# Two projection DMAs in place of four, and five stores in place of three, in a FiLM layer kernel

## Chip, cores and metric

One core of a Trainium2 chip. The metric is the device time of one execution in microseconds (us). All runs quoted are of the fast state, with a granted clock of 1.00. The same kernel differs by up to 0.4% between jobs on different chips (84.04 to 84.38 us for the kernel before), so each experiment is compared with runs of the kernel before from its own job.

## The reference

```python
# x 32 x 512 x 256, conditioning 32 x 64, gamma_proj and beta_proj 64 x 256, all float32
gamma = conditioning @ gamma_proj
beta = conditioning @ beta_proj
return (x * (1 + gamma[:, None, :]) + beta[:, None, :]).astype(np.float32)
```

It reads 16.78 MB of x and writes 16.78 MB; everything else is small.

## The kernel before

Each of the 128 partitions holds 128 rows of x (a quarter of one batch item, 128 KB). SyncE issues the loads, ScalarE issues everything else that is a DMA. VectorE takes 11 of every 16 rows, GpSimd the other 5.

```python
LOADS = {0: [8, 8, 8, 8, 32, 32, 26, 6]}
STORES = {0: (64, 96, 128)}
GROUP = 16
ON_DVE = 11
# ... (pools cut)
nc.scalar.dma_start(out=cond_s, in_=conditioning)
gbproj = consts.tile([2 * cond_dim, dim], f32)      # rows alternate: gamma, beta, gamma, ...
half = cond_dim // 2
for h, proj in enumerate((gamma_proj, beta_proj)):
    for c0 in (0, half):
        nc.scalar.dma_start(out=gbproj[2 * c0 + h : 2 * (c0 + half) : 2, :],
                            in_=proj[c0 : c0 + half, :])
# ... (the loads of x, one per entry of LOADS, on nc.sync)
# ... (conditioning transposed and repeated on PE; gb_p = gamma | beta for each partition in PSUM;
#      ScalarE copies 1 + gamma and beta to gb_s in SBUF for GpSimd)
held = consts.tile([P, 1], f32)
# ...
for r0 in range(0, ROWS, GROUP):
    # ... (v: 11 rows for VectorE, w: 5 rows for GpSimd; g_p, b_p, g_s, b_s repeated over rows)
    nc.vector.scalar_tensor_tensor(out=v, in0=rows(g_p, nv), scalar=1.0, in1=v, op0=ALU.add, op1=ALU.mult)
    nc.gpsimd.tensor_tensor(out=w, in0=w, in1=rows(g_s, nw), op=ALU.mult)
    nc.vector.tensor_add(out=v, in0=v, in1=rows(b_p, nv))
    nc.gpsimd.tensor_tensor(out=w, in0=w, in1=rows(b_s, nw), op=ALU.add)
    if s == 0 and r0 + GROUP == STORES[0][0]:
        nc.scalar.copy(out=held, in_=slabs[-1][:, ROWS - LOADS[SLABS - 1][-1] - 1, 0:1])   # the gate
    for e0, e1 in zip((0,) + STORES[s], STORES[s]):
        if r0 < e1 <= r0 + GROUP:
            nc.scalar.dma_start(out=o_v[s, :, e0:e1, :], in_=xs[:, e0:e1, :])
```

The copy to `held` reads row 121, which the load before the last one brings. It keeps ScalarE from issuing any store until then.

## Time and profile before

| what | value |
|---|---|
| time, median of 3 runs | 84.04 us (84.01 to 84.16) |
| span of the profiled run | 82.3 us |
| VectorE, GpSimd busy | 61%, 56% |
| both DMA queues together, share of 16 engines | 96.5% |
| last load packet ends, first store packet starts (trace) | 42.4 us, 42.1 us |
| last store packet ends (trace) | 81.1 us |

The prediction below shows the lines that carry this. Three lines that it uses but does not show are from the timeline (start, length, engine, line, operation, and the idle time before it with what ended it):

```profile
3.12 6.79 DMA gbproj<-in_beta_proj_dram
```

```profile
10.04 2.04 PE L94 MATMUL gb_p<-gbproj,cond_T 128*128 128x256 f32 x4 [4.37 <-DMA gbproj<-in_beta_proj_dram]
...
58.78 3.09 DVE L121 TENSOR_TENSOR xs<-xs,gb_p 128x2816 f32<-128x2816 f32 x1
```

The first is from the chain that ended last: the last projection DMA takes 6.79 us for 32 KB, since it shares the engines with loads. The second and third frame the computing: it cannot begin before gb_p, and VectorE is done at 58.78 + 3.09 = 61.87 us, 20 us before the end.

### The profile page before, as it was taken

The numbers are of one execution on the slowest core, as the hardware profiler recorded it, in microseconds if no ns is written. First come the engines' busy times: TensorE is split into PE (matmuls) and PEld (weight loads), VectorE is DVE, ScalarE is ACT, GpSimd is POOL, SyncE is SP. The second block draws the span as 40 slices with busy tenths as digits, with TensorE's granted clock in tenths as the row PEclk, the third lists the DMA queues.
The fourth block names the chain that finished last, engine by engine and source line by source line (L and its number), as shares of the span: only waits on it lengthen the run. The fifth ranks groups of instructions, "written<-read, shape, count | busy, mean of one in ns | idle before, by whom it ended". The sixth has DMA issues, their size and how long they took to land.

```text
span 82.3 us, 140 instructions
## 1 busy us (share of the span) xinstructions
PE 3.3 (4%) x8; PEld 2.1 (3%) x8; DVE 50.1 (61%) x23; ACT 2.1 (3%) x4; POOL 46.4 (56%) x22
## 2 busy tenths in 40 slices
PE   0050180000000000000000000000000000000000
PEld 0040140000000000000000000000000000000000
DVE  1040007999999999999999999999990000000000
ACT  0140012000000000000000000000000000000000
POOL 2000008999999999999999999999700000000000
DMA  2999999799889989999999928999955995998890
GB/s 48 331 426 396 401 418 597 303 462 510 382 382 510 430 350 446 414 427 414 397 689 510 510 127 382 510 510 510 510 255 255 510 510 255 510 510 382 382 510 0
DMA packets 1824, 33.69 MB, mean 409 GB/s; under 512 B 288, under 2 KB 416, under 8 KB 544
## 3 DMA queue, kind: packets, MB, share of 16 engines
q1 hardware_dynamic: 1152, 16.78, 48.7%
q10 hardware_dynamic: 672, 16.92, 47.8%
HBM read 16.92 MB, written 16.78 MB: 409 GB/s over the span
## 4 chain that ended last, share of the span: by engine, by line
DVE 52%; DMA 8%; issue 8%; ACTq 3%; PE 2%; ACT 1%
DVE xs L118 30%; DVE xs L121 23%; DMA gbproj<-in_beta_proj_dram 8%; PE gb_p L94 2%; ACTq L55 2%; ACTq L49 0%; ACT gb_s L98 0%; ACT gb_s L101 0%
## 5 line engine op out<-in xcount | busy, mean ns | idle before, releaser
L120 POOL TENSOR_TENSOR xs<-xs,gb_s 128x1280 f32<-128x1280 f32 x8 | 23.1, 2887 | 11.5 <-ACT gb_s L98 11.5
L118 DVE SCALAR_TENSOR_TENSOR xs<-gb_p,xs 128x2816 f32<-128x2816 f32 x8 | 24.7, 3084 | 6.8 <-ACT gb_s L101 6.8
L121 DVE TENSOR_TENSOR xs<-xs,gb_p 128x2816 f32<-128x2816 f32 x8 | 24.7, 3088 | 0.3
L122 POOL TENSOR_TENSOR xs<-xs,gb_s 128x1280 f32<-128x1280 f32 x8 | 23.1, 2885 | 0.6
L94 PE MATMUL gb_p<-gbproj,cond_T 128*128 128x256 f32 x4 | 2.0, 666 | 4.4 <-DMA gbproj<-in_beta_proj_dram 4.4
L82 DVE COPY wide<-cond_s 32x64 f32<-32x64 f32 x2 | 0.3, 182 | 2.8 <-DMA cond_s<-in_conditioning_dram 2.8
L84 PE MATMUL cond_T_p<-rident,wide 32*128 32x128 f32 x4 | 1.2, 456 | 4.5 <-DVE rident L72 4.5
L98 ACT ACT_TABLE_LOAD x1 | 1.3, 1283 | 3.8 <-issue 3.8
L94 PEld LDWEIGHTS gb_p<-gbproj,cond_T 128*128 128x128 f32 x4 | 1.2, 323 | 4.8 <-issue 4.6
L87 DVE COPY cond_T<-cond_T_p 128x128 f32<-128x128 f32 x2 | 0.6, 292 | 1.0 <-PE cond_T_p L84 0.9
L84 PEld LDWEIGHTS cond_T_p<-rident,wide 32*128 32x128 f32 x4 | 0.9, 319 | 4.4 <-DVE rident L72 4.4
L125 ACT COPY held<-xs 128x1 f32<-128x1 f32 x1 | 0.2, 191 | 28.2 <-DMA xs<-in_x_dram 28.2
L81 DVE MEMSET wide<- 32x128 f32 x2 | 0.3, 165 | 0.8 <-PEq L145 0.8
L98 ACT ACTIVATE gb_s<-gb_p 128x256 f32<-128x256 f32 x1 | 0.4, 383 | 7.1 <-PE gb_p L94 7.1
L101 ACT COPY gb_s<-gb_p 128x256 f32<-128x256 f32 x1 | 0.4, 367 | 0.0
masks.py:197 POOL MEMSET ident<- 32x32 f32 x1 | 0.1, 114 | 0.3 <-POOLq L145 0.3
masks.py:199 POOL TENSOR_SCALAR_AFFINE_SELECT ident<-ident 32x32 f32<-32x32 f32 x1 | 0.2, 202 | 0.1
L145 POOL MEMSET const-float32-0.0<- 128x1 f32 x1 | 0.1, 104 | 0.2 <-issue 0.2
L72 DVE COPY rident<-ident 32x128 f32<-32x128 f32 x1 | 0.2, 208 | 0.0
L145 POOL MEMSET const-bfloat16-1.0<- 128x1 bf16 x1 | 0.1, 107 | 0.0
L145 POOL MEMSET const-uint8-127<- 128x1 uint8 x1 | 0.1, 107 | 0.0
L145 POOL MEMSET const-float32-1.0<- 128x1 f32 x1 | 0.1, 104 | 0.0
## 6 DMA issues: line engine op xcount, KB each, us to landing
xs<-in_x_dram SPq DMA_DIRECT2D x2, 4096.0 KB, 22.0
out_dram<-xs ACTq DMA_DIRECT2D x2, 4096.0 KB, 20.8
xs<-in_x_dram SPq DMA_DIRECT2D x4, 1024.0 KB, 8.4
xs<-in_x_dram SPq DMA_DIRECT2D x1, 3328.0 KB, 32.9
xs<-in_x_dram SPq DMA_DIRECT2D x1, 768.0 KB, 33.9
gbproj<-in_gamma_proj_dram ACTq DMA_DIRECT2D x2, 32.0 KB, 6.0
gbproj<-in_beta_proj_dram ACTq DMA_DIRECT2D x2, 32.0 KB, 6.6
cond_s<-in_conditioning_dram ACTq DMA_DIRECT2D x1, 8.0 KB, 3.1
```

The source lines that it names most:

```text
L55: nc.scalar.dma_start(out=gbproj[2 * c0 + h : 2 * (c0 + half) : 2, :], in_=proj[c0 : c0 + half, :])
L81: nc.vector.memset(wide, 0.0)
L84: nc.tensor.matmul(t_p, lhsT=wide.rearrange("b k h -> b (k h)"), rhs=rident, start=True, stop=True)
L87: nc.vector.tensor_copy(out=t_s, in_=t_p)
L94: nc.tensor.matmul(p_t[:, h * dim : (h + 1) * dim], lhsT=cond_T[h][:, s * P : (s + 1) * P], rhs=gbproj, start=True, stop=True)
L98: nc.scalar.activation(out=s_t[:, :dim], in_=p_t[:, :dim], func=mybir.ActivationFunctionType.Identity, bias=1.0, scale=1.0)
L101: nc.scalar.copy(out=s_t[:, dim:], in_=p_t[:, dim:])
L118: nc.vector.scalar_tensor_tensor(out=v, in0=rows(g_p, nv), scalar=1.0, in1=v, op0=ALU.add, op1=ALU.mult)
L120: nc.gpsimd.tensor_tensor(out=w, in0=w, in1=rows(g_s, nw), op=ALU.mult)
L121: nc.vector.tensor_add(out=v, in0=v, in1=rows(b_p, nv))
L122: nc.gpsimd.tensor_tensor(out=w, in0=w, in1=rows(b_s, nw), op=ALU.add)
L145: nc = _bacc.Bacc("TRN2", target_bir_lowering=False, num_devices=1)
```

## The change

The intent: fewer DMAs ahead of the computing, each over all partitions, and stores in smaller pieces, so that the first can go early and the last is short.

```diff
-    STORES = {0: (64, 96, 128)}
+    STORES = {0: (32, 64, 96, 112, 128)}
...
-    half = cond_dim // 2
-    for h, proj in enumerate((gamma_proj, beta_proj)):
-        for c0 in (0, half):
-            nc.scalar.dma_start(out=gbproj[2 * c0 + h : 2 * (c0 + half) : 2, :],
-                                in_=proj[c0 : c0 + half, :])
+    nc.scalar.dma_start(out=gbproj[0::2, :], in_=gamma_proj)
+    nc.scalar.dma_start(out=gbproj[1::2, :], in_=beta_proj)
```

## The prediction

> **What bounds the kernel now.** I read the page first: busy time by engine, the DMA queues, then the chain of work that ended last.
>
> ```profile
> span 82.3 us, 140 instructions
> ...
> PE 3.3 (4%) x8; PEld 2.1 (3%) x8; DVE 50.1 (61%) x23; ACT 2.1 (3%) x4; POOL 46.4 (56%) x22
> ...
> q1 hardware_dynamic: 1152, 16.78, 48.7%
> q10 hardware_dynamic: 672, 16.92, 47.8%
> HBM read 16.92 MB, written 16.78 MB: 409 GB/s over the span
> ...
> DVE 52%; DMA 8%; issue 8%; ACTq 3%; PE 2%; ACT 1%
> ```
>
> No compute engine is full: VectorE 61%, GpSimd 56%. The two DMA queues (q1 carries the loads of x, q10 the stores, the conditioning and the projections) sum to 48.7 + 47.8 = 96.5% of the time of 16 engines. That is 79.4 of 82.3 us; the remaining 2.9 us are the start (the first read begins at about 1.8 us) and the end. The chain names VectorE with 52%, and here it misleads: it runs back from the last instruction that computes (VectorE's, which ends at 58.78 + 3.09 = 61.87 us) and says nothing of the 20 us of transfers after it.
>
> Next I asked the DMA view for stretches in which nearly all packets have one size: 43 to 61 us (the 64-row store, 64 KB a packet), 62 to 81 us (32-row stores, 32 KB), 10 to 12 us (8-row loads, 8 KB).
>
> ```profile
> DMA packets 112, 7.34 MB, mean 408 GB/s; under 512 B 0, under 2 KB 0, under 8 KB 0
> q10 hardware_dynamic: 112, 7.34, 94.2%
> out_dram<-xs ACTq DMA_DIRECT2D x1, 4096.0 KB, 22.1
> ```
>
> ```profile
> DMA packets 267, 7.86 MB, mean 414 GB/s; under 512 B 27, under 2 KB 27, under 8 KB 27
> q10 hardware_dynamic: 267, 7.86, 96.2%
> out_dram<-xs ACTq DMA_DIRECT2D x1, 4096.0 KB, 19.5
> ```
>
> ```profile
> DMA packets 119, 0.84 MB, mean 422 GB/s; under 512 B 16, under 2 KB 16, under 8 KB 16
> q1 hardware_dynamic: 119, 0.84, 101.7%
> ```
>
> Share x 16 engines x length of the stretch / packets is the time of one packet. 64 KB: 0.942 x 16 x 18 / 112 = 2.422 us. 32 KB: 0.962 x 16 x 19 / 240 = 1.218 us (267 packets less 27 tiny ones that report completion). 8 KB: 1.017 x 16 x 2 / 103 = 0.316 us. (A packet counts in the slice where it starts, hence a share above 100%, and the jagged digits of the page's DMA row, which are not pauses.) The last row of the second fence is the final store: 4 MB need 8 x 1.218 = 9.7 us of each engine, but it took 19.5 us from issue to landing. It stood about 10 us in the queue behind the store before it. So the stores were ready before the DMA engines could take them.
>
> Last, the timeline around the turn from loading to storing.
>
> ```profile
> 40.95 0.19 ACT L125 COPY held<-xs 128x1 f32<-128x1 f32 x1 [28.18 <-DMA xs<-in_x_dram]
> 41.19 21.10 ACTq L129 DMA_DIRECT2D out_dram<-xs  x3
> ```
>
> ScalarE, which issues all stores, waits 28.18 us for row 121 of x, which is in the last load but one. The stores start right after, at 41.19 us, though rows 0 to 63 were finished by 37.4 us. The copy to `held` is a gate: no store before nearly all loads are in.
>
> **What the Trainium skill says.** "DMA: Bandwidth & Descriptors", section "Issuing engines are not separate DMA queues": transfers from any issuing engine share the same 16 DMA engines and interleave. The trace agrees: the two queues together make 96.5%, never much over 100%. The same page, "Where 436 GB/s comes from": the ports allow about 435 GB/s. The trace has 32 KB in 1.218 us on each of 16 engines, 430 GB/s; this kernel is at that ceiling while it streams. "Trace Analysis", section "DMA Optimizations": splitting DMAs may let some start sooner, "If DMA engines are generally idle". Here they are not idle, so the page gives the change no gain. "DMA: Bandwidth & Descriptors", section "Rules for kernel authors": 1 MiB or more per DMA over 128 partitions for the most bandwidth. The new stores have 4, 4, 4, 2 and 2 MB, all above that.
>
> **The change part by part.**
>
> *Projections.* Two DMAs of 64 rows in place of four of 32 rows, the same 128 packets of 1 KB, from the same ScalarE queue. Removed: two issues (0.51 to 0.73 us each in the tile view of gbproj, so ScalarE is free about 1.2 us earlier) and two completion packets per engine. Before, the last of the four was issued at 3.1 us and landed at 9.9 us, because each small packet takes turns with an 8 KB load packet of 0.316 us. Per engine there were 4 x (2 data + 1 completion) = 12 turns; now there are 2 x (4 + 1) = 10. Saving about 2 x 0.32 = 0.6 us, so I put the gb_p matmuls at 9.2 to 9.5 us instead of 10.0, and VectorE's end at about 61.2 instead of 61.9 us. The gain to VectorE can be at most about 1.7 us anyway: rows 32 to 63 land at about 23.3 us (issued at 5.5, 17.8 us to landing), and VectorE takes them at 25.05 now. What is it worth at the end? Nothing: the last store has some 10 us of slack already, and the 0.13 MB of projections move either way. Fewer completion packets are worth a few tens of ns.
>
> *Loads.* Untouched in size and order. In the built kernel (the instruction order with its waits) each DMA takes one of eight completion semaphores in turn; two DMAs fewer ahead of the loads means that the fourth and fifth load need not wait for the conditioning and the first load, so SyncE issues them some us earlier. The engines had queued loads at that time (q1 at 93.8% and q10 at 8.4% from 5 to 10 us), so this moves no byte earlier.
>
> *The gate.* It moves in the source to the first store, but is still one copy that waits for row 121, and the instruction order shows it in the same place on ScalarE, ahead of all stores. So the 32-row store, ready at 25 us, still goes at about 41.2 us.
>
> *Stores.* Three become five. Per DMA engine (8 of the 128 partitions): rows 0 to 63 were 8 packets of 64 KB and become 16 of 32 KB: 16 x 1.218 - 8 x 2.422 = +0.11 us. Rows 64 to 95 stay. Rows 96 to 127 were 8 of 32 KB and become 16 of 16 KB. No 16 KB packet is in the trace; from 2.422 and 1.218 the fixed part of a packet is 0.014 us and 32 KB cost 1.204 us, so 16 KB are an estimated 0.616 us (the same line gives 0.315 for 8 KB, measured 0.316). 16 x 0.616 - 8 x 1.218 = +0.11 us. Completion packets: 16 DMAs in all before (1 + 4 + 8 + 3) and 16 after (1 + 2 + 8 + 5), no difference. Two more issues of 0.34 us on ScalarE hide under transfers.
>
> Does the queue ever run dry? With stores from 42.2 us at 9.7 us per 32 rows, it needs rows 64 to 95 by 61.7, rows 96 to 111 by 71.4, rows 112 to 127 by 76 us. VectorE has them by 49.6, 55.7 and 61.9 us. Never.
>
> Sum: 84.04 + 0.22 - up to 0.1 from the start = **84.2 us**.
>
> **The rivals.**
>
> 1. *The tail shrinks.* If the end is VectorE's end plus the last store's time, then a 2 MB store in place of 4 MB saves 5 us (half of 9.7), or 10 us if one halves the 19.5. For it: VectorE's place in the chain, and that the last store is issued when it ends. Against it: those 19.5 us are half queueing. It would make 74 to 79 us.
> 2. *Stores start earlier* and overlap with loads. For it: rows 0 to 31 are done at 25 us. Against: the gate, and DMA engines at 99.3% between 13.7 and 41 us; starting earlier would only push loads back. It would make 84 us, perhaps worse from starved compute.
> 3. *VectorE's earlier start reaches the end*: 83.4 us. Against: the 10 us of slack.
> 4. *Small packets or a queue hiccup cost more* than 12 to 14 ns each, for instance if 16 KB stores ran at 5% less: 0.5 us on 9.7, making 84.7 us. The 8 KB loads on the line of the others speak against.
>
> **Range and chances.** The mechanism leaves only tenths of a us. Runs of before span 84.01 to 84.16. I take 83.9 to 84.6: the low end allows a somewhat cleaner start, the high end rival 4. A move of 2% (1.7 us) either way needs rival 1, or a stall that no view shows: 1% each.
>
> **What would show it.** Right: queue shares still sum to about 96%, with 16 KB packets near 0.616 us and 32 KB ones at 1.218; the `held` copy again near 41 us and the first store straight after; gb_p matmuls 0.5 to 1 us earlier; VectorE's end earlier with the span unchanged; the last store taking well over its own 4.9 us (an estimate, 8 x 0.616) to land, some 20 us. Wrong: a last store that lands about 5 us after its issue (rival 1), store packets among the loads before 40 us (rival 2), stretches of the storing stage with fewer packets in flight, or loads that end later than 42.9 us because the early issue of loads holds up something.

## The result, and the profile after

The changed kernel took 84.05 us (median of 6 runs, 83.93 to 84.16), the kernel before in the same rounds 84.11 us (6 runs, 84.01 to 84.31). The ratio is 0.999, with a 95% interval of 0.9973 to 1.0007: the same. A ratio here is the mean time of one kernel's fast runs over that of the other's of the same rounds, so it is not quite the ratio of the medians.

The page of the changed kernel, with the queue lines that answer to those of before (packets, MB, share of 16 engines' span):

```profile
span 82.3 us, 141 instructions
...
q1 hardware_dynamic: 1152, 16.78, 48.3%
q10 hardware_dynamic: 928, 16.92, 48.2%
```

The sum is 96.5% again, but it is made up differently. The loads' queue fell from 48.7 to 48.3% (0.4% of 82.3 us = 0.33 us), the stores' queue rose from 47.8 to 48.2%, by the same amount. 256 more packets (928 against 672) are 16 more on each DMA engine.

The DMA view of 71 to 81 us, where only the new 16 KB packets run:

```profile
DMA packets 302, 4.19 MB, mean 419 GB/s; under 512 B 46, under 2 KB 46, under 8 KB 46
...
q10 hardware_dynamic: 302, 4.19, 98.7%
```

0.987 x 16 x 10 us / 256 packets = 0.617 us for one of 16 KB, where 0.616 was estimated. The queue is full to the end.

The timeline, with the rows that answer to those shown of before:

```profile
9.10 2.05 PE L91 MATMUL gb_p<-gbproj,cond_T 128*128 128x256 f32 x4 [3.41 <-DMA gbproj<-in_beta_proj_dram]
...
40.70 0.19 ACT L122 COPY held<-xs 128x1 f32<-128x1 f32 x1 [28.87 <-DMA xs<-in_x_dram]
...
57.85 3.09 DVE L118 TENSOR_TENSOR xs<-xs,gb_p 128x2816 f32<-128x2816 f32 x1
```

gb_p comes 0.94 us earlier and VectorE ends 0.93 us earlier, at 60.94 us. The gate opens at 40.70 instead of 40.95 us; the first store follows at 40.92 us. The span does not move. And the last store, issued at 61.0 us (DMA view of 60.5 to 61.5 us; operation, KB, us from issue to landing):

```profile
out_dram<-xs ACTq DMA_DIRECT2D x1, 2048.0 KB, 20.4
```

It has half the bytes of the last store before, and lands no sooner after its issue (19.5 us then): it queues for some 15 us.

The trace's own packet records show where the two terms lie. The last load packet ends at 42.12 us instead of 42.36 us, so loading ends 0.24 us earlier. From the first store packet to the last it is 39.29 instead of 39.01 us, so storing takes 0.28 us longer. The two cancel. These are single traces: in all six with three stores this length is 39.0 to 39.1 us, in the two with five stores and undelayed computing 39.2 and 39.3 us, so the stores' term is about 0.2 us.

Why loading got shorter is in the DMA view of 6 to 9 us, when the projections' 1 KB packets run between the 8 KB packets of the loads. Before, then after:

```profile
DMA packets 294, 1.19 MB, mean 396 GB/s; under 512 B 64, under 2 KB 161, under 8 KB 161
```

```profile
DMA packets 287, 1.28 MB, mean 428 GB/s; under 512 B 48, under 2 KB 142, under 8 KB 142
```

Fewer bytes were moved in these 3 us before. In the packet records 84 of the 8 KB packets took 0.33 to 0.39 us before, between 6.5 and 9.2 us, in place of 0.31 us. After, none in that time is over 0.33 us.

### The profile page after: what moved, and what is told of

It is laid out like the page before. It is cut to its first block, busy times and chain, and to the rows that moved or that the text cites. A ratio compares the mean times of both kernels' runs of the same rounds, so it can differ in the third digit from the quotient of the medians.

```text
span 82.3 us, 141 instructions
## 1 busy us (share of the span) xinstructions
PE 3.3 (4%) x8; PEld 2.1 (3%) x8; DVE 50.1 (61%) x23; ACT 2.1 (3%) x4; POOL 46.4 (56%) x22
## 3 DMA queue, kind: packets, MB, share of 16 engines
q1 hardware_dynamic: 1152, 16.78, 48.3%
q10 hardware_dynamic: 928, 16.92, 48.2%
## 4 chain that ended last, share of the span: by engine, by line
DVE 52%; DMA 9%; issue 8%; PE 3%; ACTq 1%; ACT 1%
DVE xs L115 30%; DVE xs L118 23%; DMA gbproj<-in_beta_proj_dram 9%; PE gb_p L91 3%; ACTq L52 1%; ACTq L49 0%; ACT gb_s L95 0%; ACT gb_s L98 0%
## 5 line engine op out<-in xcount | busy, mean ns | idle before, releaser
L117 POOL TENSOR_TENSOR xs<-xs,gb_s 128x1280 f32<-128x1280 f32 x8 | 23.1, 2888 | 10.5 <-ACT gb_s L95 10.5
```

## The experiments

My theory after the result: the DMA engines are full, so only their work counts. The five stores add 0.2 to 0.3 us of packets, the new projection DMAs take 0.2 to 0.3 us of packet time away, and VectorE's earlier end is lost in slack. Rivals: nothing in it matters and the agreement is chance; VectorE's end counts; the last store's length counts; the number of DMAs, not where they land, matters in the projections.

### Each part alone

The new projections with the old stores:

```diff
-    STORES = {0: (32, 64, 96, 112, 128)}     # of the changed kernel
+    STORES = {0: (64, 96, 128)}
```

> The new projection DMAs with the old three stores. Theory (two small terms of opposite sign cancel in the change): the loading stage ends about 0.24 us earlier, because the lengthened 8 KB load packets between 6.5 and 9.2 us disappear, and the stores keep their old packets, so the total is about 0.24 us below before, ratio 0.996 to 0.998; gb_p matmuls near 9.1 us, VectorE's end near 60.9 us, q1 share 48.3%, q10 share 47.8%. Rival (the projections are worth nothing and the agreement of the two kernels is just noise): ratio 1.000, q1 share 48.7%. Rival (VectorE's 0.9 us reach the end): ratio 0.989.

Measured: 84.18 us (6 runs) against 84.38 us, ratio 0.9985 (0.997 to 1.000). gb_p at 9.25 us, VectorE's end at 61.1 us, queue shares 48.5 and 47.8%. The direction is as expected and the size is a little under; the interval just touches 1. The rival of 0.989 is ruled out.

The new stores with the old projections:

```diff
-    STORES = {0: (64, 96, 128)}              # of the kernel before
+    STORES = {0: (32, 64, 96, 112, 128)}
```

> The five stores with the old four projection DMAs. Theory: 16 more packets on each DMA engine at 14 ns, so the storing stage is 0.22 us longer and nothing pays for it: about 0.2 us above before, ratio 1.002 to 1.004; q10 share 48.2%, q1 share 48.7%; gb_p matmuls stay at 10.0 us. Rival (the last store's length sets the end): 74 to 79 us. Rival (the change is worth nothing in either part): ratio 1.000.

Measured: 84.60 us (5 runs) against 84.38 us, ratio 1.0036 (1.0023 to 1.0049). The five stores alone cost 0.3 us, and this is clear of noise. gb_p stays at 10.2 us. The q1 share was 48.6% of 82.9 us, the q10 share 47.8% (I had expected 48.2%: a share of a longer span). The finer stores are a small loss, hidden in the change by the projections' small gain. The two ratios multiply to 1.0021, a little above the interval of the whole change (0.9973 to 1.0007). So the times alone, from different jobs, do not show how exactly the two parts cancel; that reading rests on the packet records as well.

### Is it the number of projection DMAs, or where they land?

Four DMAs, each over all partitions, in the kernel before:

```diff
-        for c0 in (0, half):
-            nc.scalar.dma_start(out=gbproj[2 * c0 + h : 2 * (c0 + half) : 2, :],
-                                in_=proj[c0 : c0 + half, :])
+        for j in (0, 1):
+            nc.scalar.dma_start(out=gbproj[2 * j + h :: 4, :], in_=proj[j::2, :])
```

> Four projection DMAs as before, but each over all 128 partitions (every fourth row) in place of one half of them. It tells two causes of the lengthened 8 KB load packets apart (85 to 91 of them between 6.5 and 9.2 us in the kernels with split projections, about 0.2 us of each DMA engine; none in those with merged ones). Theory A (spreading over all partitions cures it): no 8 KB packet over 0.33 us after 4 us, mean of the 8 KB packets 0.323 to 0.330 us, ratio to before about 0.998. Theory B (the number of small DMAs, with their issues and completion packets, causes it): some 85 lengthened packets as before, mean 0.333 to 0.341, ratio 1.000. Both: gb_p matmuls stay at about 10 us, as there are still 12 turns.

And two DMAs, each over one half of the partitions, with three stores (the conditioning is laid out to match, the result is the same):

```diff
-    nc.scalar.dma_start(out=gbproj[0::2, :], in_=gamma_proj)
-    nc.scalar.dma_start(out=gbproj[1::2, :], in_=beta_proj)
+    nc.scalar.dma_start(out=gbproj[:cond_dim, :], in_=gamma_proj)
+    nc.scalar.dma_start(out=gbproj[cond_dim:, :], in_=beta_proj)
...
-        wide = consts.tile([batch, cond_dim, 2], f32, name=f"wide{h}")
+        wide = consts.tile([batch, 2, cond_dim], f32, name=f"wide{h}")
...
-        nc.vector.tensor_copy(out=wide[:, :, h], in_=cond_s)
+        nc.vector.tensor_copy(out=wide[:, h, :], in_=cond_s)
...
-        nc.tensor.matmul(t_p, lhsT=wide.rearrange("b k h -> b (k h)"), rhs=rident,
+        nc.tensor.matmul(t_p, lhsT=wide.rearrange("b h k -> b (h k)"), rhs=rident,
```

> Two projection DMAs of 64 rows, but gamma on partitions 0 to 63 and beta on 64 to 127 (the conditioning is laid out to match; the result is the same), with the three stores of before. Theory A (the spread over all partitions matters): lengthened 8 KB packets are back, some 80 of them, ratio about 1.000. Theory B (the number of DMAs matters): none, ratio about 0.998. Both: gb_p matmuls near 9.2 us.

The DMA view of 6 to 9 us of these two, first four DMAs over all partitions, then two over halves:

```profile
DMA packets 307, 1.25 MB, mean 417 GB/s; under 512 B 67, under 2 KB 167, under 8 KB 167
```

```profile
DMA packets 278, 1.15 MB, mean 384 GB/s; under 512 B 48, under 2 KB 150, under 8 KB 150
```

With four DMAs over all partitions no 8 KB packet is lengthened in that stretch and the time is 83.98 us against 84.27 us, ratio 0.9969 (0.9953 to 0.9985). With two over halves 78 packets are lengthened and it is 84.42 us, ratio 1.0018 (1.0003 to 1.0033). So it is where the rows land, and not how many DMAs there are. The count shows in the latency, and so does the place: gb_p came at 9.82 us with four DMAs over all partitions, at 9.52 us with two over halves, and at 9.10 us with two over all, as in the change.

All eleven traces whose first loads are of 8 rows agree: 84, 85, 91, 87 and 78 lengthened packets in the five where a projection DMA covers one half of the partitions, none in the six (one of them without the gate, see below) where it covers all. Leaving out the one without the gate, whose loads run otherwise, the last load packet ends at 42.36 to 42.62 us (mean 42.50) with halves and at 42.12 to 42.30 us (mean 42.24) without. The term is 0.26 us.

One page of the Trainium skill may bear on this: "SBUF — State Buffer", section "Door 1: The DMA port swizzle", says that partitions 0 to 63 reach only 8 of the 16 ports through which DMA reaches that memory. A projection DMA on one half could then crowd 8 ports that the loads use too. That ports are the cause is not shown. The records name no port. The lengthening begins 1.0 to 1.7 us after the first projection packet, and then it takes every load packet: with two halves, all 16 that start between 6.4 and 6.8 us took 0.326 us or more, though fewer than 64 of the 128 projection packets had started, so that little but gamma's half was being written. Crowding of 8 ports alone would seem to spare the packets for the other half of the partitions. So the place of the rows is shown as the cause, and the way it acts stays open.

### How much slack does VectorE have, and do finer stores change it?

Four spare VectorE instructions ahead of the main loop, 12.4 us of lateness, on an unused tile. First in the kernel before:

```diff
     held = consts.tile([P, 1], f32)
+    spare = consts.tile([P, ON_DVE, dim], f32)
+    nc.vector.memset(spare, 0.0)
...
+            for _ in range(4):
+                nc.vector.scalar_tensor_tensor(out=spare, in0=rows(g_p, ON_DVE), scalar=1.0, in1=spare,
+                                               op0=ALU.add, op1=ALU.mult)
             for r0 in range(0, ROWS, GROUP):
```

> The kernel before, with four spare VectorE instructions on an unused tile ahead of the main loop, 4 x 3.08 = 12.3 us, so VectorE ends at about 74.2 us. Theory (VectorE has about 10 us of slack with three stores, and the stores run dry beyond it): the last store of 32 rows is issued at 74.2 us, moves 1.1 us later, needs 9.75 us of each DMA engine: end about 4 us later, 88 us in all, with an idle gap of the DMA engines of about 2.5 us before it. Rival (VectorE's end sets the time now): 12.3 us more, 96 us. Rival (slack is larger, DMA alone counts): 84.1 us.

Measured: 92.83 us (4 runs) against 84.38 us, ratio 1.102. A miss: 8.5 us later, not 4. The timeline of ScalarE in this run shows why:

```profile
41.10 0.19 ACT L130 COPY held<-xs 128x1 f32<-128x1 f32 x1 [28.25 <-DMA xs<-in_x_dram]
49.91 24.84 ACTq L134 DMA_DIRECT2D out_dram<-xs  x3
```

The gate opened at 41.10 us, but the first store was issued at 49.91 us, when VectorE had finished row 63. I had looked at the last store only. In the table by stretch (stretch, its length, busy time of PE, PEld, DVE, ACT and POOL, clock, DMA share, GB/s) the DMA engines stand idle between loads and stores:

```profile
42.50:50.80 8.30, 0.00 (x0) 0.00 (x0) 8.27 (x4) 0.00 (x0) 8.14 (x4) 1.00 0.09 39
50.80:90.00 39.20, 0.00 (x0) 0.00 (x0) 23.39 (x8) 0.00 (x0) 8.34 (x3) 1.00 0.97 420
```

So the slack of the kernel before is that of its first store: 41.2 - 37.4 = 3.8 us from the last VectorE instruction for row 63 to the gate. Lateness beyond it goes straight to the end: 12.4 - 3.8 = 8.6 us, measured 8.5.

That corrected reading was tested with two spare instructions in place of four (6.2 us):

> The kernel before with two spare VectorE instructions, 6.2 us of lateness. It tests the reading of e3_late_three_stores, whose time was mis-forecast: it is the first store, of rows 0 to 63, that runs out of slack, with 41.2 - 37.4 = 3.8 us from VectorE's row 63 to the gate. Expected from that: 6.2 - 3.8 = 2.4 us later, 86.4 to 86.9 us, ratio about 1.028, first store issued at about 43.6 us. Rival (slack is the 10 us of the last store, as I had it): 84.3 us.

Measured: 86.43 us (4 runs) against 84.26 us, ratio 1.026, which is 2.2 us where 2.4 was expected; the first store was issued at 43.59 us. The reading holds.

The same four spare instructions in the changed kernel:

> The changed kernel with the same four spare VectorE instructions, 12.3 us, VectorE's end at about 73.3 us. Theory: with five stores the last piece is needed only at about 76 us, and rows 64 to 95 come about 0.6 us too late for the queue (done at 61.0, needed at 61.5 less 1.1 us for the issue): about 84.7 us, so the finer stores buy tolerance of late computing and no time as the kernel stands. Rival (the finer stores make no difference to anything): 88 us as with three stores, less the 0.9 us of the earlier start.

Measured: 84.76 us (4 runs) against 84.38 us in the same job, ratio 1.0047 (1.0031 to 1.0063). VectorE ended at 70.31 + 3.09 = 73.4 us:

```profile
70.31 3.09 DVE L123 TENSOR_TENSOR xs<-xs,gb_p 128x2816 f32<-128x2816 f32 x1
```

```profile
40.87 0.19 ACT L127 COPY held<-xs 128x1 f32<-128x1 f32 x1 [28.95 <-DMA xs<-in_x_dram]
41.09 32.73 ACTq L131 DMA_DIRECT2D out_dram<-xs  x5
```

The first store, of 32 rows, went at 41.09 us as ever. In the packet records the DMA engines stand idle once while they store, for 0.6 us each up to 62.07 us, ahead of rows 64 to 95: the gap that was expected. 12 us of late computing that cost the kernel before 8.5 us cost the changed one about half a us (ratio 1.0047 against 0.999, from different jobs). Up to 0.9 us of the difference is VectorE's earlier start; the rest is what the finer stores buy. The kernel as it stands has no late computing to spend it on.

### Is the gate what hides the early stores?

```diff
-                if s == 0 and r0 + GROUP == STORES[0][0]:
-                    nc.scalar.copy(out=held, in_=slabs[-1][:, ROWS - LOADS[SLABS - 1][-1] - 1, 0:1])
```

> The changed kernel without the copy that holds all stores back until row 121 has landed, so the first 32-row store goes at about 24 us and shares the DMA engines with the loads. Theory (the DMA engines are full in any order, so order moves no time): 83.9 to 84.6 us, loads end at about 59 us instead of 42, VectorE ends at about 68 us with waits for loads. Rival 2 of the prediction (early stores gain): under 83 us. Rival (reads and writes in turn cost the DMA engines time, or the late rows come too late to be stored): over 85.5 us.

Measured: 84.69 us (4 runs) against 84.27 us, ratio 1.0065 (1.0038 to 1.0093). This is just above the 84.6 us that I had allowed. The first store was issued at 24.47 us and its first packet moved at 29.0 us, in place of 40.9 and 41.8 us. So a first store that is issued 16 us earlier gains nothing; this loses about 0.6 us on the changed kernel (1.0065 against 0.999, from different jobs). The loads give way, and the last VectorE multiplication waits for them:

```profile
67.32 3.09 DVE L115 SCALAR_TENSOR_TENSOR xs<-gb_p,xs 128x2816 f32<-128x2816 f32 x1 [5.32 <-DMA xs<-in_x_dram]
```

VectorE ended at 73.5 us; I had said 68, and loads lasted until 66.9 instead of 59 us, both too early. The 32 KB load packets took 1.250 us on average in place of 1.218 us and the longest 1.86 us, which over 16 packets per engine is 0.5 us. That does not account for the loss by itself: in the same trace the store packets took 0.25 us less per engine than in the changed kernel, and the first 8 KB loads 0.3 us more. Why loads take longer and stores less time when the two alternate is open.

### What does a packet cost?

Sixteen stores of 8 rows in the changed kernel (the gate is kept, ahead of the first):

```diff
-    STORES = {0: (32, 64, 96, 112, 128)}
+    STORES = {0: tuple(range(8, 129, 8))}
...
-                if s == 0 and r0 + GROUP == STORES[0][0]:
+                if s == 0 and r0 == 0:
```

> The changed kernel with sixteen stores of 8 rows, 8 KB a packet. Theory (each packet costs a fixed 0.014 us beside its bytes): per DMA engine 128 x 0.315 = 40.3 us of packets in place of 39.1, and 11 more completion packets of 0.009 us: 1.3 us above the changed kernel, about 85.3 us, ratio to before 1.013 to 1.018. Rival (packets of 8 KB and more cost only their bytes): 84.1 us. Rival (the issues of 0.34 to 1.06 us on ScalarE or the eight completion semaphores hold the queue up): over 86.5 us with idle DMA slices in the storing stage.

Measured: 85.44 us (4 runs) against 84.27 us, ratio 1.0137 (1.0122 to 1.0152). The DMA view of 43 to 81 us:

```profile
DMA packets 2185, 15.93 MB, mean 419 GB/s; under 512 B 240, under 2 KB 240, under 8 KB 240
...
q10 hardware_dynamic: 2185, 15.93, 101.1%
```

1.011 x 16 x 38 us / 1945 packets = 0.316 us for 8 KB, as was computed for the loads between 10 and 12 us, and there is no idle time between them. So a fixed part of 14 ns a packet fits this larger number of stores too. It is not the same for every load: in the packet records the 8 KB loads from 4 to 6 us, before anything lengthened them, took 0.309 us.

### A version to beat both

Merged projections, loads of 16 rows at the start, four stores:

```diff
-    LOADS = {0: [8, 8, 8, 8, 32, 32, 26, 6]}
-    STORES = {0: (32, 64, 96, 112, 128)}
+    LOADS = {0: [16, 16, 32, 32, 26, 6]}
+    STORES = {0: (32, 64, 96, 128)}
```

> A candidate to beat both: merged projections, first loads of 16, 16, 32 rows in place of four of 8 and a 32, stores ending at 32, 64, 96, 128 rows. Theory: 16 packets of 8 KB fewer per DMA engine, 16 x 0.014 us = 0.2 us less, 0.1 us more for the first stores of 32 rows than with 64, and 0.15 to 0.25 us less from the projections: ratio to before 0.996 to 0.999. The projections must then take turns with packets of 16 KB, so gb_p comes at about 14 us and VectorE ends at about 66 us, 5 us later than in the changed kernel, which costs nothing as the stores have the slack. Rival (the late computing shows): over 85 us.

Measured: 84.06 us (5 runs) against 84.26 us, ratio 0.9975 (0.9961 to 0.9989). It is faster than the kernel before by 0.2 us, but no better than the kernel before with spread projections alone (0.9969 with four DMAs, 0.9985 with two); the intervals overlap. gb_p came at 11.8 us, earlier than the 14 I had expected, and VectorE's end at 63.6 us did no harm. The gain of fewer packets did not show: the 16 KB load packets took 0.654 us on average, over the 0.617 us of the stores, mostly in the slow first packets of the kernel (up to 1.49 us; from 4 us on they took 0.611 us). None of these kernels is more than about 0.3% faster than the kernel before.

## Why the prediction was right

- **The bound.** "No compute engine is full", and the queues fill 96.5%: right. The share stayed at 96.5% after the change, and a delay of VectorE by 12 us in the changed kernel cost about half a us. (The page that the prediction calls "Trace Analysis" has the title "Perfetto Trace Analysis".)
- **The stores' term, +0.22 us.** Right: 0.28 us more between the first and last store packet in the trace (about 0.2 us over all traces), and a ratio of 1.0036 (0.3 us) with this part alone. The 16 KB packet was estimated at 0.616 us and measured at 0.617.
- **The projections' latency.** 10 turns in place of 12 put gb_p at 9.2 to 9.5 us; it came at 9.10. VectorE ended at 60.9 us (expected 61.2), and this was worth nothing, as said.
- **"Up to 0.1 from the start"** is the term that was mis-sized: 0.24 us between the two traces, 0.26 us over ten. I put down the saving to completion packets ("worth a few tens of ns"). What runs showed in its place is that a projection DMA on one half of the partitions lengthens some 80 load packets, and one over all does not. The total stayed in the range because the term is small. The forecast of 84.2 us lies 0.1 us above the 84.11 us of the kernel before, and the measured 84.05 us lies 0.06 us below it: the mis-sized term accounts for most of that.
- **The slack.** "The last store has some 10 us of slack" was true and beside the point: the first store of the kernel before has only 3.8 us. With the forecast of 88 us for the delayed kernel this cost a miss (92.8 us). The change moves no computing later, so the prediction itself did not rest on it.
- **Rivals 1 and 3** (the tail, VectorE's earlier start) fell with the last store's 20.4 us to landing and an unmoved span. **Rival 2** fell to the gate, and without the gate to the full DMA engines (ratio 1.0065). **Rival 4**: packets of 16 and 8 KB kept to the line of the larger ones.

## What to carry to other kernels

When both DMA queues together fill the 16 engines from first load to last store, count the packets and bytes of each engine first. In this kernel a finer or earlier store then gained nothing, however it looked on the computing side, and cost 0.2 to 1.2 us. Finer stores bought tolerance of late computing, and the first store, not the last, was the one with the least slack. Let a small DMA that runs beside large ones cover all partitions rather than one half; here that was worth about 0.26 us.

## What the Trainium skill lacked or had wrong

- "SBUF — State Buffer", section "The DMA setup-cost knee": it holds against small transfers that each pays about 2 us. In a full queue this does not add up: sixteen stores of 1 MB in place of five cost 1.2 us in all (ratio 1.0137 against 0.999), and they moved at 419 GB/s, where the page has about 341 GB/s for one transfer of 1 MB.
- "DMA: Bandwidth & Descriptors", section "Measured (HBM→SBUF, 128 partitions, SWDGE, issued from GpSimd)": it gives about 10.5 ns a packet as the floor of a 4 KB transfer. It lacks a measured figure of this kind for large packets: here stores of 8 to 64 KB a packet fit 14 ns beside 37.6 ns per KB.
- "SBUF — State Buffer", section "Door 1: The DMA port swizzle": it tells what a transfer to one half loses itself. It lacks a figure for what that does to others: projection DMAs of 32 or 64 KB on one half lengthened 78 to 91 load packets of another queue from 0.309 us to between 0.344 and 0.360 us on average, and loading ended 0.26 us later. That its ports are the reason is not shown.
- No page has the growth of the issue time: the issue of a 128-partition store on ScalarE took 0.34 to 0.37 us alone, but 1.06 us when it followed directly on another store (the second of the five), and 0.9 to 1.2 us each in a row of twelve of 1 MB.
